# Residual additions moved to VectorE and four groups of tiles moved to other memory in a one-layer decoder step

## The chip, the cores and the metric

The kernel runs on one core of a Trainium2 chip. The metric is the device time of one execution in microseconds (us). A core has TensorE (PE, the matrix engine, whose weight loads are listed as PEld), VectorE (DVE), ScalarE (ACT), GpSimd (POOL) and SyncE (SP, which here only issues DMAs). Each engine works through its own queue in order, and an instruction that waits holds up everything behind it on that queue.

## The reference, cut to what matters

One layer of a decoder is computed for 1024 prompt rows and 64 sample rows (1088 rows of 1024 values). The parts around the change are the end of the mixer and the feed-forward block:

```python
x = x + rms_norm(merged @ w_out, norm_mix_post)          # first residual addition
h = rms_norm(x, norm_ffn_pre)
a = h @ w_ffn_a                                          # DFF = 4096 columns
ctx = concatenate([conv_buf, a], axis=1)                 # conv_buf: 2 rows of state
c = conv_b + sum(ctx[:, j:j + T] * conv_w[j] for j in range(3))
y = (silu(c) * (h @ w_ffn_b)) @ w_ffn_d
x = x + rms_norm(y, norm_ffn_post)                       # second residual addition
# the last two rows of ctx are outputs too: p_ffn_conv (prompt) and s_ffn_conv (8 samples)
```

All products are in float32 quality: each operand is split into a high and a low part, and three matmuls (high x high, low x high, high x low) make one product.

## The kernel before

`phase1` and `phase2` compute the three branches of the mixer and their merged sum, which is left as split tiles (`act_h`, `act_l`). `phase3`, `ffn`, `down_group` and `down` hold what the change touches. SBUF memory is given out by pools that are stacked from two sides. When a pool is closed, a later pool gets its memory, and a tile of the later pool waits for the last readers of the tiles that lay there. A pool with `bufs=n` gives out n copies of a tile in rotation. The order of the instructions on each queue is not the order of the program: a planner chooses it when the program is built (`schedule_with_timeline_sim=True`), by its own estimate of when each instruction is ready. Instructions that use a pool's tiles come, in that order, behind the instructions that use the pools whose memory it takes.

**The first weight rows.** `phase3` multiplies the merged sum by `w_out`. Its 8 blocks of 128 weight rows (k = 0 to 7) are loaded on SP (L1413) and split in two by `split` (L143 on ScalarE for the high part, L144 on VectorE for the low part). The raw rows of k = 0 and 1 go to `w_raw`, a tile with 2 copies in a pool (`wp`) that lives through the whole kernel. Those of k = 2 to 7 go to `pn_x` and `pn_y`, 2 copies each, of the pool `xp`. This pool takes memory in which the merged sum `macc` of `phase2` lay.

**The rows of the mixer's output.** The output is made in 9 tiles of rows, in the order 0 and 2 together, 1, 3, 4, 6, 5, 7, 8 (tile 8 holds the 64 sample rows). `sums` makes the matmuls of a tile (L1428, into `ps_u`, `ps_n`, `ps_d`), `norms` the rest: x is loaded into `pn_x` (L1439), squares are summed on ScalarE (L1443), `rstd` makes the factor (L160 to L165), VectorE multiplies (L1448), the residual is added (L1449), the row is stored (L1450), normalized again (L1452, L1454), and transposed on TensorE (L1459, read back at L1462). The two additions of a tile are on GpSimd for the tiles 0 to 6 and on VectorE for 7 and 8. The normalized x is written over the loaded x, so that a copy of `pn_x` is free for the next load only after the transposes.

**The up products and the state copies.** `ffn` makes both up products (L1628), in 16 steps of two column blocks, and writes their product to memory as `yd`. `down_first` loads and splits the first two blocks of the last product (weights L1733, y L1734). After the last step, two calls of `down_group` multiply these (L1782; the sample rows at L1774; L1788 adds to the sums, `act_h` and `act_l`). Then the state rows (`tail`) are transposed on TensorE (L1721), copied five times by VectorE into `tailT`, which has one copy (L1723), and stored by DMAs that GpSimd issues (L1724).

**The last product.** `down` opens the pool `dp`, which takes the memory of the closed pools of the up products. Its groups are one of 2 blocks (2 and 3) and seven of 4 blocks. `prep` gives a block its tiles and calls `down_part` (load the raw weight rows to `w_raw`, load y to `y_raw`, split both). For odd groups, the first one among them, y goes to `act_h1`/`act_l1`, and the first two blocks' weights go to `w_hi`/`w_lo`, which also hold the weights of blocks 0 and 1. For even groups y goes to `yh`/`yl` and the weights to `wd`, all of `dp`. `y_raw`, `gbf` and `sel` are always of `dp`. When the last group has finished a tile of 128 rows, `rows_done` makes the final norm of it (L1820 to L1825), the second residual addition (L1826; GpSimd for the prompt tiles 0 to 6, VectorE for the samples and tile 7) and the store.

Of the kernel before, what the change touches and what calls it, by code (L numbers as in the profile page):

```python
# [17 lines left out]
F32 = mybir.dt.float32  # L18
# [7 lines left out]
P = 128  # L26
D = 1024
SEQ = 1024
SB, ST = 8, 8
NS = SB * ST  # L30
# [89 lines left out]
class Builder:  # L120
# [1265 lines left out]
    def phase3(self, early):  # L1386

        tc, nc, I, O = self.tc, self.nc, self.I, self.O
        PS = bass.MemoryType.PSUM
        with ExitStack() as es:  # L1390
# [17 lines left out]
            wpt = lambda n, d=F32R: flat(self.wp.tile([P, 8, P], d, name=n))  # L1408
            wt = [wo.tile([P, D], F32R, name="w_row", bufs=10) for _ in range(10)]
            wk = []  # L1410
            for k in range(8):
                raw = wpt("w_raw", F32) if k < 2 else xp.tile([P, D], F32, name=("pn_x", "pn_y")[k % 2])
                self.shift_caches(nc.sync.dma_start(raw, I["w_out"][0][k * P:(k + 1) * P]))  # L1413
                wk.append((wpt("w_hi"), wpt("w_lo")) if k < 2 else wt[2 * (6 - k):2 * (6 - k) + 2] if k < 7 else (wpt("w_raw"), wpt("w_raw")))
                self.split(*wk[k], raw)
# [17 lines left out]
            def norms(i, ps, R, half):  # L1433

                a, e = ROWT[i]
                rows = e - a
                add = nc.vector if i >= 7 else nc.gpsimd
                x = xp.tile([P, D], F32, name="pn_x")[:rows]
                nc.sync.dma_start(x, self.xrows(a, e))  # L1439
                y = xp.tile([P, D], F32, name="pn_y")[:rows]  # L1440
                ss = self.sm.tile([P, 2], F32, name="pn_ss")[:rows]
                for u in range(2):
                    nc.scalar.activation(y[:, :512], ps[u], AF.Square, accum_out=ss[:, u:u + 1])  # L1443
                nc.vector.tensor_add(ss[:, 0:1], ss[:, 0:1], ss[:, 1:2])
                r = self.rstd(ss[:, 0:1], rows, D)
                for u in range(2):
                    v = slice(u * 512, (u + 1) * 512)
                    nc.vector.scalar_tensor_tensor(y[:, v], ps[u], r, gb[:rows, v], op0=ALU.mult, op1=ALU.mult)  # L1448
                    add.tensor_add(y[:, v], y[:, v], x[:, v])  # L1449
                nc.gpsimd.dma_start(self.x1d[a:e], y)  # L1450
                s2 = self.sm.tile([P, 1], F32, name="nrm_ss")[:rows]
                nc.scalar.activation(x, y, AF.Square, accum_out=s2)  # L1452
                r = self.rstd(s2, rows, D)
                nc.scalar.activation(x, y, AF.Copy, scale=r)  # L1454
                for c in range(8):
                    if c % 4 == 0:
                        pt = self.next_bank()
                    p = pt[:, c % 4 * P:c % 4 * P + rows]
                    nc.tensor.transpose(p, x[:, c * P:(c + 1) * P], self.ident[:rows, :rows])  # L1459
                    g = self.vec[:, VR_FFN + c:VR_FFN + c + 1]  # L1460
                    dst, src = (R[:, c], p.rearrange("p (h n) -> p h n", h=2)) if half is None else (R[:, c, half], p)
                    nc.scalar.activation(dst, src, AF.Copy, scale=g)  # L1462
# [7 lines left out]
            for j, (i, ps, _) in enumerate(tiles):  # L1470
                norms(i, ps, R02, j)
# [3 lines left out]
            for i, pl, nm in order:  # L1475
                ps, step = sums(i, pl, nm)
# [174 lines left out]
    def ffn(self, es, eu, pool, fs, stT):  # L1651
        tc, nc, I, O = self.tc, self.nc, self.I, self.O
# [4 lines left out]
        fp = pool(eu, "fp", 4)  # L1657
        W = SEQ + 2 + SB * 10
# [54 lines left out]
        self.down_start(pc)  # L1713
        for _ in range(2):
            self.down_group([self.aready.popleft()])
        for (j0, n, dst) in ((0, 2, O["p_ffn_conv"][0, 0]), (2, 16, O["s_ffn_conv"][0].rearrange("b j f -> (b j) f"))):
            d2 = dst.rearrange("j (r p) -> (j r) p", p=P)
            for a in range(0, n, 4):
                w = min(4, n - a)
                ps = self.down_bank()  # L1720
                nc.tensor.transpose(ps[:32 * w, :P], tail[:, j0 + a:j0 + a + w].rearrange("p j f -> p (j f)"), self.ident)  # L1721
                t = fs.tile([P, P], F32, name="tailT", bufs=1)
                nc.vector.tensor_copy(t[:32 * w], ps[:32 * w, :P])  # L1723
                nc.gpsimd.dma_start(d2[32 * a:32 * (a + w)], t[:32 * w])  # L1724
        eu.close()
        self.down(es, pool)

# [63 lines left out]
    def down(self, es, pool):  # L1791
        tc, nc, I, O = self.tc, self.nc, self.I, self.O
        dp = pool(es, "dp", 1, side="right")
        gb = dp.tile([P, D], F32, name="gbf")
        nc.sync.dma_start(gb, I["norm_ffn_post"][0].partition_broadcast(P))
        sel = dp.tile([P, NS], F32, name="sel")
        nc.vector.tensor_add(sel, self.ident[:, :NS], self.ident[:, NS:])
        held = {}

        def prep(g, j, fb):  # L1800

            if g % 2:
                if j == 0:
                    held[g] = [self.actp.tile([P, 4, D], F32R, name=f"act_{x}1") for x in "hl"]
                y = tuple(t[:, j] for t in held[g])
            else:
                y = tuple(dp.tile([P, D], F32R, name=n, bufs=4) for n in ("yh", "yl"))
            w = (self.wtile(self.wp, "w_hi"), self.wtile(self.wp, "w_lo")) if g % 2 and j < 2 else \
                tuple(dp.tile([P, D], F32R, name="wd", bufs=12) for _ in range(2))
            ys = dp.tile([P, 2, NS], F32R, name="ys", bufs=9)  # L1810
            return self.down_part(fb, self.wtile(self.wp, "w_raw", F32), w, dp.tile([P, NT], F32, name="y_raw", bufs=2), y, ys)

        def rows_done(src, rows, r0, dst, add):

            x, y = (t[:rows, len(done) % 4] for t in held["end"])
            done.append(r0)
            nc.sync.dma_start(x, self.x1d[r0:r0 + rows])
            ss = self.sm.tile([P, 2], F32, name="pn_ss")[:rows]
            for u in range(2):
                nc.scalar.activation(y[:, u * 512:(u + 1) * 512], src(u), AF.Square, accum_out=ss[:, u:u + 1])  # L1820
            nc.vector.tensor_add(ss[:, 0:1], ss[:, 0:1], ss[:, 1:2])  # L1821
            r = self.rstd(ss[:, 0:1], rows, D)
            for u in range(2):
                v = slice(u * 512, (u + 1) * 512)
                nc.vector.scalar_tensor_tensor(y[:, v], src(u), r, gb[:rows, v], op0=ALU.mult, op1=ALU.mult)  # L1825
                add.tensor_add(y[:, v], y[:, v], x[:, v])  # L1826
                nc.sync.dma_start(dst[:, v], y[:, v])

        done = []

        def samples_done():
            held["end"] = [self.actp.tile([P, 4, D], F32, name=f"act_{x}1") for x in "hl"]
            s = [dp.tile([P, 512], F32, name=f"smp{u}") for u in range(2)]
            fin = []
            for u in range(2):
                nc.scalar.activation(s[u], self.smp[u], AF.Copy)
                ps = self.down_bank(4)[:NS]
                nc.tensor.matmul(ps, sel, s[u], start=True, stop=True)
                fin.append(ps)
            rows_done(lambda u: fin[u], NS, SEQ, O["y_sample"].rearrange("b t d -> (b t) d"), nc.vector)  # L1840
        groups = [(2, 3)] + [tuple(range(a, a + 4)) for a in range(4, NFB, 4)]
        grp = [prep(1, j, fb) for j, fb in enumerate(groups[0])]
        for g, _ in enumerate(groups, 1):
            nxt = []
            todo = deque(groups[g] if g < len(groups) else ())

            def after(i):
                for _ in range(1 if len(grp) == 4 else 2):
                    if i % 2 == 0 and todo:
                        nxt.append(prep(g + 1, len(nxt), todo.popleft()))  # L1850
                if g == len(groups):
                    acc = self.acc[i]
                    rows_done(lambda u: acc[:, u * 512:(u + 1) * 512], P, i * P, O["y_prompt"][0, i * P:(i + 1) * P],
                              nc.vector if i == 7 else nc.gpsimd)
            self.down_group(grp, after, samples_done if g == len(groups) else lambda: None)
            grp = nxt

# [30 lines left out]
```

## Time and profile before

| what | us |
|---|---|
| median of 3 runs | 2800.94 (2800.14 to 2802.79) |
| the execution that was profiled | 2808.87 |
| its span in the profile | 2807.0 |

The profile describes one execution. Its times are counted from the start of the span. In a timeline row the columns are start, duration, engine (SPq is SP's queue), line, operation, output and inputs, shape and count; a bracket at the end tells how long the engine was idle before and what ended that. Rows with a count above 1 are merged, and their duration is that of the whole. TensorE's matmuls of 512 columns start some 0.23 us apart at its full clock.

### The profile page before, as it was taken

Reading aid. Unit: us, or ns where it says so; the run is one execution under the profiler, and the core shown is the slowest. Engines: PE = TensorE matmul, PEld = TensorE weight load, DVE = VectorE, ACT = ScalarE, POOL = GpSimd, SP = SyncE. Lnnn points to the kernel's source line nnn. Section 1 sums busy time; section 2 is a strip of 40 time slices with the busy share of each in tenths; the row PEclk is TensorE's granted clock in tenths of the full one; section 3 lists DMA queues with packets and bytes.
Section 4 is the critical chain, followed back from the end, with each engine's and each line's share of the span. In section 5 each row is a group of like instructions: output and inputs, shape, how many; then the busy total and the mean of one; then the engine's idle time right before and its main releaser. Section 6 shows DMA issues by size and latency. Waiting matters only on the chain. (4 is left out here: it accounts for less than half of the span.)

```text
span 2807.0 us, 45540 instructions
## 1 busy us (share of the span) xinstructions
PE 2661.6 (95%) x17822; PEld 2398.1 (85%) x17822; DVE 1651.0 (59%) x3944; ACT 1097.0 (39%) x2036; POOL 238.0 (8%) x367
## 2 busy tenths in 40 slices
PE   7989999899899999999999967999999999799998
PEld 6978888787787989999899747999999999588886
DVE  6346657557565754535358247777777777653435
ACT  5224526435355544444513355333333333221212
POOL 2110010000100000000000120100100100000002
PEclk9999999999999999999999988999999999899999
DMA  7456776867766333232475332332332332431303
GB/s 224 126 178 177 188 213 187 217 177 187 210 182 177 100 112 100 77 101 76 150 248 192 127 108 68 130 115 91 115 114 76 99 99 78 136 124 62 123 32 128
DMA packets 344552, 380.72 MB, mean 136 GB/s; under 512 B 57068, under 2 KB 295076, under 8 KB 343417
## 3 DMA queue, kind: packets, MB, share of 16 engines
q1 hardware_dynamic: 321808, 311.13, 36.8%
q0 software_dynamic: 22240, 65.63, 7.3%
q8 instruction: 140, 2.29, 0.3%
q10 hardware_dynamic: 288, 1.05, 0.1%
q14 instruction: 76, 0.61, 0.1%
HBM read 302.07 MB, written 123.46 MB: 152 GB/s over the span
## 5 line engine op out<-in xcount | busy, mean ns | idle before, releaser
L244 PE MATMUL ps_d<-act_h,w_hi 128*128 128x512 f32 (+2 forms) x1920 | 648.9, 338 | 8.3 <-DVE proj L832 6.8
L244 PE MATMUL ps_d<-act_l,w_hi 128*128 128x512 f32 (+2 forms) x1920 | 650.3, 339 | 0.0
L244 PE MATMUL ps_d<-act_h,w_lo 128*128 128x512 f32 (+2 forms) x1920 | 646.1, 337 | 0.0
L244 PEld LDWEIGHTS ps_d<-act_h,w_hi 128*128 128x128 f32 x1920 | 367.7, 192 | 37.1 <-DVE proj L832 7.5
L244 PEld LDWEIGHTS ps_d<-act_l,w_hi 128*128 128x128 f32 x1920 | 367.8, 192 | 30.0 <-issue 3.8
L244 PEld LDWEIGHTS ps_d<-act_h,w_lo 128*128 128x128 f32 x1920 | 367.6, 191 | 28.0 <-issue 2.8
L143 ACT ACTIVATE w_hi<-w_raw 128x1024 fp32r<-128x1024 f32 (+1 forms) x156 | 140.5, 903 | 275.2 <-PE ps_d L244 184.6
L144 DVE TENSOR_TENSOR w_lo<-w_raw,w_hi 128x1024 fp32r<-128x1024 f32 (+1 forms) x124 | 138.4, 1118 | 117.1 <-ACT w_hi L143 115.4
L1066 DVE CUSTOM_DVE_ANT_0 qb<-kc,qb 128x128 f32<-128x128 f32 x384 | 89.3, 287 | 101.2 <-DMA qb<-qrow 86.5
L1628 PE MATMUL ps_u<-Yh,w_hi 128*128 128x288 f32 (+1 forms) x512 | 103.7, 292 | 6.0 <-ACT Yh L143 6.0
L1628 PE MATMUL ps_c<-Yh,wx 128*128 128x288 f32 (+1 forms) x512 | 106.3, 289 | 0.0
L1628 PE MATMUL ps_u<-act_h,w_lo 128*128 128x288 f32 (+1 forms) x512 | 104.7, 289 | 1.0 <-DVE rs_v L160 1.0
L1628 PE MATMUL ps_d<-act_h,w_hi 128*128 128x288 f32 (+1 forms) x512 | 104.6, 293 | 0.7 <-DVE pn_y L1448 0.7
L1628 PE MATMUL ps_u<-Yh,wx 128*128 128x288 f32 (+1 forms) x512 | 102.4, 289 | 0.0
L1628 PE MATMUL ps_d<-act_h,w_lo 128*128 128x288 f32 (+1 forms) x512 | 101.6, 288 | 0.1
L1628 PE MATMUL ps_c<-act_h,wx 128*128 128x288 f32 (+1 forms) x512 | 101.4, 288 | 0.0
L244 PE MATMUL ps_d<-ohi,w_hi 128*128 128x256 f32 (+2 forms) x288 | 94.3, 329 | 2.5 <-ACT proj L1144 1.4
L244 PE MATMUL ps_d<-olo,w_hi 128*128 128x320 f32 (+2 forms) x288 | 94.6, 328 | 0.0
L244 PE MATMUL ps_d<-ohi,w_lo 128*128 128x320 f32 (+2 forms) x288 | 94.1, 327 | 0.0
L1144 ACT ACTIVATE proj<-ps_d,nbin 128x512 f32<-128x512 f32 (+2 forms) x96 | 53.3, 555 | 94.9 <-PE ps_d L244 94.9
L143 ACT ACTIVATE wx<-S 128x512 fp32r<-128x512 f32 x64 | 40.4, 632 | 124.9 <-PE ps_c L1628 124.9
L1628 PEld LDWEIGHTS ps_u<-Yh,w_hi 128*128 128x128 f32 x512 | 83.7, 192 | 6.2 <-ACT Yh L143 6.2
(638 smaller groups left out, 6365.6 us busy)
## 6 DMA issues: line engine op xcount, KB each, us to landing
w_raw<-in_w_in SPq DMA_DIRECT2D x80, 512.0 KB, 4.1
out_s_win<-in_cache_win_kv SPq DMA_DIRECT2D x40, 1016.0 KB, 7.0
kc<-in_cache_win_kv SPq DMA_DIRECT2D x80, 256.0 KB, 3.8
qb<-qrow SPq DMA_DIRECT2D x64, 256.0 KB, 4.8
kc<-in_cache_win_kv SPq DMA_DIRECT2D x128, 128.0 KB, 3.3
w_raw<-in_w_ffn_a SPq DMA_DIRECT2D x32, 512.0 KB, 3.8
w_raw<-in_w_ffn_b SPq DMA_DIRECT2D x32, 512.0 KB, 3.6
yd<-ext POOLq DMA_DIRECT2D x32, 512.0 KB, 4.8
```

What stands on the lines that cost most here:

```text
L143: self.nc.scalar.activation(hi, src, AF.Copy)
L144: self.nc.vector.tensor_sub(lo, src, hi.bitcast(F32))
L244: nc.tensor.matmul(ps, W[:, c], X(c), start=n == 0, stop=n == 3 * kb - 1)
L1066: nc.vector.tensor_tensor_reduce(q[:, j], k[:, j], q[:, j], 1.0, 0.0, ALU.mult, ALU.add, T[:, c:c + 1])
L1144: self.proj(col, lambda ps, a, e: nc.scalar.activation(y[:, a:e], ps, AF.Exp, bias=nb, scale=-1.0))
L1628: nc.tensor.matmul(p, w[:, c], self.side_b(t, b, x, c), start=new and m == 0, stop=m == 11, skip_group_check=not new)
```

## The change

It does four things. (1) The additions L1449 and L1826 are on VectorE for all tiles. (2) The raw rows of k = 2 and 3 of `w_out` go to `w_raw`. (3) The state copies go to five column ranges of one tile `ext` of the pool `fp`, whose four copies served the up products. (4) In `prep` the odd and even groups change roles, so that the first group's y and weights go to `yh`/`yl` and `wd` of `dp`, and the last group's to `act_h1`/`act_l1`; `rows_done` then takes `yh`/`yl` in place of parts of `act_h1`/`act_l1`.

```diff
-                raw = wpt("w_raw", F32) if k < 2 else xp.tile([P, D], F32, name=("pn_x", "pn_y")[k % 2])
+                raw = wpt("w_raw", F32) if k < 4 else xp.tile([P, D], F32, name=("pn_x", "pn_y")[k % 2])
...
-                add = nc.vector if i >= 7 else nc.gpsimd
...
-                    add.tensor_add(y[:, v], y[:, v], x[:, v])
+                    nc.vector.tensor_add(y[:, v], y[:, v], x[:, v])
...
+        tails = fp.tile([P, W], F32, name="ext")
+        o = 0
...
-                t = fs.tile([P, P], F32, name="tailT", bufs=1)
-                nc.vector.tensor_copy(t[:32 * w], ps[:32 * w, :P])
-                nc.gpsimd.dma_start(d2[32 * a:32 * (a + w)], t[:32 * w])
+                t = tails[:32 * w, o:o + P]
+                o += P
+                nc.vector.tensor_copy(t, ps[:32 * w, :P])
+                nc.gpsimd.dma_start(d2[32 * a:32 * (a + w)], t)
...
-            if g % 2:
+            if g % 2 == 0:
                 if j == 0:
                     held[g] = [self.actp.tile([P, 4, D], F32R, name=f"act_{x}1") for x in "hl"]
                 y = tuple(t[:, j] for t in held[g])
             else:
                 y = tuple(dp.tile([P, D], F32R, name=n, bufs=4) for n in ("yh", "yl"))
-            w = (self.wtile(self.wp, "w_hi"), self.wtile(self.wp, "w_lo")) if g % 2 and j < 2 else \
+            w = (self.wtile(self.wp, "w_hi"), self.wtile(self.wp, "w_lo")) if g % 2 == 0 and j < 2 else \
                 tuple(dp.tile([P, D], F32R, name="wd", bufs=12) for _ in range(2))
...
-            x, y = (t[:rows, len(done) % 4] for t in held["end"])
-            done.append(r0)
+            x, y = (dp.tile([P, D], F32, name=n, bufs=4)[:rows] for n in ("yh", "yl"))
...
-                add.tensor_add(y[:, v], y[:, v], x[:, v])
+                nc.vector.tensor_add(y[:, v], y[:, v], x[:, v])
```

## Rows read from the trace of the kernel before

**Rows 1.** The page: busy time, share of the span and instructions of each engine.
```profile
PE 2661.6 (95%) x17822; PEld 2398.1 (85%) x17822; DVE 1651.0 (59%) x3944; ACT 1097.0 (39%) x2036; POOL 238.0 (8%) x367
```

**Rows 2.** Stretches: us, busy PE, PEld, DVE, ACT, POOL, granted clock, DMA share, GB/s.
```profile
1661.00:1690.00 29.00, 11.33 (x51) 8.66 (x50) 21.84 (x46) 20.20 (x52) 9.90 (x6) 0.65 0.53 188
...
2412.50:2425.00 12.50, 0.05 (x1) 0.00 (x0) 2.25 (x5) 3.48 (x5) 1.10 (x2) 0.64 0.56 182
2425.00:2441.00 16.00, 11.01 (x26) 7.50 (x27) 9.24 (x13) 5.66 (x9) 1.62 (x3) 0.54 0.54 183
...
2757.00:2795.00 38.00, 37.80 (x167) 30.96 (x165) 29.96 (x66) 12.64 (x43) 17.87 (x12) 1.00 0.47 153
```

**Rows 3.** Timeline of DVE, SP, ACT and PE at the first weight rows.
```profile
1535.93 1.22 DVE L144 TENSOR_TENSOR w_lo<-w_raw,w_hi 128x1024 fp32r<-128x1024 f32 x1
1544.47 1.23 DVE L144 TENSOR_TENSOR w_lo<-w_raw,w_hi 128x1024 fp32r<-128x1024 f32 x1
...
1546.16 0.33 SPq L1405 DMA_DIRECT2D gb<-in_norm_mix_post  x1
1546.54 0.42 SPq L1413 DMA_DIRECT2D pn_x<-in_w_out  x1
...
1552.21 1.06 ACT L143 ACTIVATE w_row<-pn_x 128x1024 fp32r<-128x1024 f32 x1 [7.22 <-DMA pn_x<-in_w_out]
...
1553.32 0.79 PE L1428 MATMUL ps_u<-w_row,act_h 128*128 128x512 f32 x1 [4.25 <-ACT w_row L143]
1558.18 0.63 PE L1428 MATMUL ps_d<-w_row,act_l 128*128 128x512 f32 x1
1560.54 0.40 PE L1428 MATMUL ps_u<-w_row,act_l 128*128 128x512 f32 x1
```

**Rows 4.** Timeline of POOL, PE and DVE at the first residual additions.
```profile
1607.94 2.53 POOL L1449 TENSOR_TENSOR pn_y<-pn_y,pn_x 128x512 f32<-128x512 f32 x2 [21.05 <-DMA pn_x<-in_x_prompt]
1628.32 3.28 POOL L1449 TENSOR_TENSOR pn_y<-pn_y,pn_x 128x512 f32<-128x512 f32 x2 [16.99 <-DVE act_l L144]
1665.16 6.26 POOL L1449 TENSOR_TENSOR pn_y<-pn_y,pn_x 128x512 f32<-128x512 f32 x2 [25.47 <-DVE w_lo L144]
1679.64 2.52 POOL L1449 TENSOR_TENSOR pn_y<-pn_y,pn_x 128x512 f32<-128x512 f32 x2 [7.36 <-DVE pn_y L1448]
...
1679.40 0.69 PE L1459 MATMUL ps_t<-ident,pn_x 128*128 128x128 f32 x2 [12.50 <-ACT pn_x L1454]
...
1688.68 1.29 DVE L1449 TENSOR_TENSOR pn_y<-pn_y,pn_x 128x512 f32<-128x512 f32 x2 [0.25 <-DMA pn_x<-in_x_prompt]
```

**Rows 5.** Timeline of SP, ACT, DVE and PE at the start of the last product.
```profile
2414.20 0.33 SPq L1733 DMA_DIRECT2D w_raw<-in_w_ffn_d  x1
2414.69 1.05 SPq L1795 DMA_DIRECT2D gbf<-in_norm_ffn_post  x1
2415.83 0.86 SPq L1734 DMA_DIRECT2D y_raw<-yd  x2
...
2411.86 1.06 ACT L143 ACTIVATE w_hi<-w_raw 128x1024 fp32r<-128x1024 f32 x1 [9.65 <-issue]
2423.94 1.06 ACT L143 ACTIVATE act_h<-y_raw 128x1024 fp32r<-128x1024 f32 x1 [4.35 <-DMA y_raw<-yd]
...
2424.71 0.29 DVE L1723 COPY tailT<-ps_c 128x128 f32<-128x128 f32 x1 [7.84 <-DMA out_s_ffn_conv<-tailT]
2432.38 1.22 DVE L144 TENSOR_TENSOR act_l<-y_raw,act_h 128x1024 fp32r<-128x1024 f32 x1
...
2425.05 0.80 PE L1782 MATMUL ps_d<-w_hi,act_h 128*128 128x512 f32 x1 [12.50 <-DVE tailT L1723]
2433.66 0.79 PE L1782 MATMUL ps_d<-w_hi,act_l 128*128 128x512 f32 x1 [2.74 <-DVE act_l L144]
```

**Rows 6.** The last rows: sums by line, then timeline rows of PE and DVE.
```profile
L1821 DVE TENSOR_TENSOR pn_ss<-pn_ss 128x1 f32<-128x1 f32 x8 | 6.9, 868 | 3.3 <-ACT act_l L1820 3.3
L165 DVE TENSOR_TENSOR rs_r<-rs_r,rs_u 128x1 f32<-128x1 f32 x8 | 1.3, 159 | 0.3
...
2794.41 0.39 PE L1782 MATMUL ps_c<-wd,yh 128*128 128x512 f32 x1
2797.23 0.68 DVE L1788 TENSOR_TENSOR act_l<-act_l,ps_c 128x512 f32<-128x512 f32 x1
```

More of the change, by code (lines that the diff above doesn't have):

```diff
@@ L1811, in prep, with rows_done @@
             return self.down_part(fb, self.wtile(self.wp, "w_raw", F32), w, dp.tile([P, NT], F32, name="y_raw", bufs=2), y, ys)
-        def rows_done(src, rows, r0, dst, add):
-            x, y = (t[:rows, len(done) % 4] for t in held["end"])
-            done.append(r0)
+        def rows_done(src, rows, r0, dst):
+            x, y = (dp.tile([P, D], F32, name=n, bufs=4)[:rows] for n in ("yh", "yl"))
             nc.sync.dma_start(x, self.x1d[r0:r0 + rows])
@@ L1825, in rows_done @@
                 nc.vector.scalar_tensor_tensor(y[:, v], src(u), r, gb[:rows, v], op0=ALU.mult, op1=ALU.mult)
-                add.tensor_add(y[:, v], y[:, v], x[:, v])
+                nc.vector.tensor_add(y[:, v], y[:, v], x[:, v])
                 nc.sync.dma_start(dst[:, v], y[:, v])
-        done = []
         def samples_done():
-            held["end"] = [self.actp.tile([P, 4, D], F32, name=f"act_{x}1") for x in "hl"]
             s = [dp.tile([P, 512], F32, name=f"smp{u}") for u in range(2)]
@@ L1839, in samples_done @@
                 fin.append(ps)
-            rows_done(lambda u: fin[u], NS, SEQ, O["y_sample"].rearrange("b t d -> (b t) d"), nc.vector)
+            rows_done(lambda u: fin[u], NS, SEQ, O["y_sample"].rearrange("b t d -> (b t) d"))
         groups = [(2, 3)] + [tuple(range(a, a + 4)) for a in range(4, NFB, 4)]
@@ L1852, in after @@
                     acc = self.acc[i]
-                    rows_done(lambda u: acc[:, u * 512:(u + 1) * 512], P, i * P, O["y_prompt"][0, i * P:(i + 1) * P],
-                              nc.vector if i == 7 else nc.gpsimd)
+                    rows_done(lambda u: acc[:, u * 512:(u + 1) * 512], P, i * P, O["y_prompt"][0, i * P:(i + 1) * P])
             self.down_group(grp, after, samples_done if g == len(groups) else lambda: None)
```

## The prediction, made before the changed kernel ran

> **What bounds the kernel now.** I read the page first. TensorE is busy for 2661.6 of 2807.0 us [rows 1], so it sets the time nearly everywhere and an edit pays only where TensorE stands still or runs at its lower clock. The page's slices and then the table of stretches show that this happens where one stage hands over to the next. I then went through TensorE's timeline for its idle brackets and followed each to what released it. Three hand-overs and the end of the kernel lie in the code that changes.
>
> At the first weight rows TensorE has used up the blocks k = 0 and 1 of w_out and waits 4.25 us for block 2 [rows 3]. Its raw rows were asked for at 1546.54, behind gb at 1546.16, because both lie where the merged sum lay, and landed shortly before ScalarE's split at 1552.21. After the wait TensorE is at its lower level (1.2 GHz): from 1553.32 to 1558.60 it does 12 matmuls 0.43 us apart, where 0.23 is the full pace.
>
> In the rows of the mixer's output TensorE waits 12.50 us for the normalized x of tile 6 [rows 4], and in the stretch 1661 to 1690 it is busy for 11.33 of 29 us, while VectorE is for 21.84 and ScalarE for 20.20 [rows 2].
>
> At the start of the last product it waits 12.50 us, and again 2.74 us [rows 5]; two more waits between them make 2.2 us. In 2425 to 2441 it does 26 matmuls, at a clock of 0.54 [rows 2], which at 0.23 us each are 6.0 us of work. So the hand-over loses 12.5 + (16 - 6.0) = 22.5 us. Two things cause it. The y of the first group is asked for at 2415.83, because SP stood until 2414.20 at a weight load (that of block 5) whose raw tile was not split before 2411.86, which in turn had to wait for the products of block 1 to let go of w_hi and w_lo. And VectorE copies the state rows through one tile: each copy waits for the store of the one before, up to 7.84 us, so that the low part of y comes only at 2432.38 [rows 5].
>
> At the end the last matmul is over at 2794.80, and VectorE adds it to the sums only at 2797.23 [rows 6]; 9.8 us of norm and store follow, up to the span's end.
>
> **The change part by part.** *First weight rows.* Block 2 can now be loaded once block 0 is split, at 1535.93 + 1.22 = 1537.15, and block 3 from 1544.47 + 1.23 = 1545.70 [rows 3]. No other load is displaced on SP: the next one, gb, is issued at 1546.16 anyhow. Block 2 then lies ready before TensorE wants it at about 1549.1, and its matmuls for three row tiles (18 at 0.23, 4.1 us) last to 1553.2. Block 3 is issued ahead of gb, and if it takes as long as block 2 did (1546.54 to 1552.21, 5.7 us) it can be split from 1551.4, the high part by 1552.5. Gone are the 4.25 us and 12 x (0.43 - 0.23) = 2.4 us: **6.6**. Bounds: 2.5, if block 3 lands 4 us late, and 6.6.
>
> *First additions.* Fourteen additions on GpSimd, 2.5 us for most pairs, become as many on VectorE at 1.29 a pair [rows 4]. Where TensorE has other work (tiles 0, 2, 1) I cost them at nothing: sums of later tiles cover them; without that cover it would be 1.29 each. On the path is tile 6. Its pair took 6.26 us, because VectorE was busy beside it, and the 12.50 us wait follows from it; with 1.29 up to 5.0 go. What is late next is the factor, which already stands in the queues of ScalarE and VectorE among splits of the up weights, so I take 3.0. Tile 5's pair gives back 0.7 (the two products and additions take 2.7 together, where they took 3.4), tile 3's 0.3. Together **4**. Bounds: -3 (VectorE has 7 x 1.2 = 8.4 us more, of which I let a third fall on the path, since it is busy for three quarters of 1661 to 1690) and 8. Whenever an addition waits for its x, all that is queued on VectorE waits too: factors, products that free PSUM banks, splits. I cost that at nothing since the pair of tile 7, which is on VectorE already, waited 0.25 us [rows 4].
>
> *State copies.* Each copy costs VectorE 0.29 us [rows 5] and none waits for a store, so five end some 1.5 us after the transposes, about 2414, instead of at 2430. The tile's own memory held products whose stores were issued by 2391, so nothing hides there.
>
> *First group.* Its weights and y are now tiles of dp. In the trace whatever uses dp (y_raw, gbf, sel, wd) stands behind the last state copy on its queue, so the low splits of all four tiles come after 2414: 4 x 1.2 us, the last at 2419. Block 3's weights can still not be early: by the pools' sizes they fall on tiles that hold y of block 1 until about 2411.6. But nothing stands before the y loads on SP any more, since the weight loads of blocks 4 and 5 now come after these splits. The y loads can then start while blocks 0 and 1 are still multiplied, and y's high part is due at about 2414.5 on ScalarE. TensorE is idle from 2412.55 to then, 2.0 us, and some 3.0 more until the low parts are there; 0.5 to 1.5 for a lower clock. That leaves 6.5 of 22.5: **16**. The second group must be ready earlier too. Before, its y loads were spread over 16 us; now they start that much earlier, and VectorE has 6 blocks' splits (6 x 2.4) and 16 sums (16 x 0.6), 24 us, in the 26 us up to 2440. It just fits. Bounds: 5, if the y loads still land after 2422 and only the later waits and the lower clock go, and 20.
>
> *Last additions.* Seven pairs, 8.4 us, go to VectorE, which is busy for 29.96 of 38 us there [rows 2]. In return the small sum L1821 has its way free: it takes 0.87 us on average beside GpSimd's additions, where the like operation L165 takes 0.16 [rows 6], so 8 x 0.7 = 5.7 us go. The net 2.7 us can fall into VectorE's idle time (it waits for ScalarE several times a tile), and then the 2.4 us lag at the end shrinks, or they can come on top. I take a gain of **1**, between -2.7 and 3. The Trainium skill says, in SBUF — State Buffer, section Who interferes with whom, that a VectorE instruction with two SBUF inputs and a GpSimd instruction that reads SBUF exclude each other, the later one waiting in full; rows 6 agree, and by that rule alone the term would be 0.7 for the last tile. Its page Perfetto Trace Analysis, section Optimizing Scalar/DVE Operations, speaks against the edit: a saturated VectorE may be relieved by handing work to GpSimd. By that the term would be -2.7.
>
> The sum is 6.6 + 4 + 16 + 1 = 27.6. Against the profiled execution (2808.87, of which 2807.0 is the span and 1.9 lies around it) that is 2781.3. This execution is 7.9 us above the median of the runs shown; taken off their median, 2800.94, it is **2773.3**, rounded to 2774. With all lower ends the gain is 2.5 - 3 + 5 - 2.7 = 1.8 (2799), with all upper ones 37.6 (2763).
>
> **The rivals.** *The last product's hand-over stays.* For: block 3's weights are bound as before, and every split of the first group now stands behind the copies. If the y loads are placed behind gbf or the copies' stores, they land as late as before, after 2422. Against: SP no longer meets a load that waits for a split. Then this term is 5, the additions and the end are 0, and the gain is 11.6: 2789.
>
> *VectorE stands in the waits for x.* GpSimd's additions waited 21.05, 16.99 and 25.47 us for their x [rows 4], 63.5 in all, and it cost nobody anything. If the planner, expecting x earlier, puts an addition ahead of ready work, VectorE waits in its place. The place is tiles 3 and 6, after which TensorE has no sums left to cover: 17.0 + 25.5 = 42.5 us, against the 23.6 of the other terms: 2800.94 - 23.6 + 42.5 = 2820. It decides once more than 27 us of these waits are met. Against: the wait of 0.25 us at tile 7.
>
> *The edits do little.* If the planner's new order opens as much elsewhere as it closes, the time is within 5.6 us of 2801; I see no row for it.
>
> **How the numbers follow.** Forecast, 2766 to 2781: 0.66. Hand-over stays, 2782 to 2794: 0.18. VectorE in the waits, 2807 or more: 0.07. Little: 0.04. More than forecast (upper ends), below 2766: 0.05. A measurement of this kernel can tell some 0.2%, 5.6 us, from no change. So faster 0.89, same 0.04, slower 0.07. The range 2764 to 2792 takes in the forecast, most of the first rival and part of the upper ends, and leaves out less than 0.2.
>
> **What would show it.** Right: no wait above 1 us at block 2 of w_out, and a clock of 1.0 there; tile 6's wait below 10 us; the first y loads of dp issued before 2412 on the old time scale, state copies some 0.3 us apart, TensorE's wait before the first group below 4 us; L1821 near 0.16 us. Wrong: VectorE rows at L1449 with brackets of 10 us or more that a load of pn_x ended; y_raw loads still issued after the copies; a new wait at the second group; the last VectorE sum more than 3 us behind the last matmul.

## The result and the profile after

The changed kernel takes 2769.62 us (median of 4 runs, 2768.37 to 2774.73) beside 2801.86 for the kernel before in the same runs: a ratio of 0.9884, with a 95% interval of 0.9864 to 0.9904. The forecast was 2774, between 2764 and 2792. A second series of the same kernel (below) gave 0.9899 (0.9881 to 0.9917). The two differences are 32.2 and 27.0 us. The profiled execution took 2770.02 us, 2767.8 of it the span.

The page's busy times of the changed kernel, to be laid beside [rows 1]:

```profile
PE 2652.2 (96%) x17822; PEld 2391.7 (86%) x17822; DVE 1654.2 (60%) x3972; ACT 1096.3 (40%) x2036; POOL 196.2 (7%) x339
```

TensorE does the same 17822 matmuls in 9.4 us less busy time, and its share rises from 95% to 96%. The rest is idle time that went. GpSimd loses its 28 additions.

Five stages can be cut out of TensorE's timeline by its own rows: up to the first product of w_out, from there to the first product of the up weights with Yh (Yh and Yl are the high and low part of differences of the normalized rows; the product stands behind a wait of 5.6 to 7.1 us that ScalarE's Yh ends), to the end of the up products, to the last matmul, and to the span's end. In the two profiled executions:

| stage, us | before | after | difference |
|---|---|---|---|
| up to the first product of w_out | 1538.77 | 1531.19 | -7.6 |
| w_out and the norms, up to the Yh products | 183.44 | 170.72 | -12.7 |
| up products | 666.22 | 666.63 | +0.4 |
| last product | 406.37 | 388.14 | -18.2 |
| after the last matmul | 12.20 | 11.12 | -1.1 |

The first stage is no part of the change: TensorE's order of work is the same there in all kernels of this study. Over its 14 profiled executions that stage varies from 1527.78 to 1541.41 us. The stages behind it repeat far better, and this is why the experiments are read stage by stage. In the kernels that leave a stage unedited, w_out and the norms take 182.3 to 183.4 (five kernels, mean 182.9), the last product 403.4 to 406.4 (five, mean 404.7), the tail, which is the stage after the last matmul, 12.1 to 12.2 (five). Four traces hold the changed kernel's w_out and norms as they are: 170.55, 170.72, 170.89 and 172.46. By the means of the unedited kernels the change gains 12.2 + 16.5 + 1.1 - 0.4 = 29.4 us, and the forecast's sum was 27.6.

The stretches of after, in the columns of [rows 2]. The first is the start of w_out, with the same stretch of before beneath it; the others answer to those of [rows 2]:

```profile
1531.19:1561.91 30.72, 30.72 (x139) 25.03 (x138) 11.84 (x16) 10.27 (x15) 0.00 (x0) 1.00 0.56 218
...
1646.00:1675.00 29.00, 12.73 (x65) 9.27 (x63) 25.26 (x55) 22.17 (x61) 1.60 (x3) 0.71 0.58 199
2392.67:2405.17 12.50, 9.31 (x40) 7.38 (x41) 9.63 (x16) 6.53 (x10) 2.69 (x5) 1.00 0.70 245
2405.17:2421.17 16.00, 16.00 (x72) 13.19 (x71) 15.97 (x24) 9.36 (x14) 0.00 (x0) 1.00 0.84 272
2718.88:2756.88 38.00, 37.80 (x163) 30.24 (x162) 30.93 (x75) 13.10 (x44) 0.00 (x0) 1.00 0.47 156
```
```profile
1538.77:1569.49 30.72, 26.47 (x108) 21.14 (x107) 11.90 (x15) 8.96 (x10) 0.00 (x0) 0.89 0.58 221
```

At w_out TensorE is never idle any more, and does 139 matmuls where it did 108. In the rows of the mixer's output it still stands for more than half the stretch, now with VectorE busy for 25.26 of 29 us. At the last product's start the clock stays at 1.00, where it was 0.64 and 0.54.

### The profile page after: what moved, and what is told of

The parts are those of the page before. It is cut to its first block, busy times and chain, and to the rows that moved or that the text cites. A ratio compares the mean times of both kernels' runs of the same rounds, so it can differ in the third digit from the quotient of the medians.

```text
span 2767.8 us, 45536 instructions
## 1 busy us (share of the span) xinstructions
PE 2652.2 (96%) x17822; PEld 2391.7 (86%) x17822; DVE 1654.2 (60%) x3972; ACT 1096.3 (40%) x2036; POOL 196.2 (7%) x339
## 4 chain that ended last, share of the span: by engine, by line
PE 79%; DMA 7%; issue 7%; DVE 3%; ACT 2%; SPq 1%; POOL 0%; DVEq 0%; POOLq 0%; ACTq 0%
PE ps_d L244 30%; PE ps_u L1627 10%; PE ps_c L1627 7%; PE ps_d L1627 7%; PE ps_u L1784 4%; PE ps_d L1784 4%; PE ps_c L1784 4%; DMA qb<-qrow 2%; DMA kt<-kb 1%; PE ps_d L1428 1%; PE ps_u L1428 1%; PE ps_n L1428 1%; PE ps_c L1776 1%; DMA kc<-in_cache_win_kv 1%; DMA comb<-ocomb 1%
## 5 line engine op out<-in xcount | busy, mean ns | idle before, releaser
L244 PEld LDWEIGHTS ps_d<-act_h,w_lo 128*128 128x128 f32 x1920 | 367.4, 191 | 27.6 <-issue 2.5
```

The lines of the kernel that those rows point to most:

```text
L244: nc.tensor.matmul(ps, W[:, c], X(c), start=n == 0, stop=n == 3 * kb - 1)
```

## The experiments

All kernels below are timed against the kernel before in the same runs, and each was profiled once. Behind "Measured" stands the ratio of the times with its 95% interval, then the lengths of stages from the one trace; "the mean" is that of the unedited kernels above.

**Which of the two edits opens the last product?** One kernel has the state copies alone, one the exchange of odd and even groups alone, one both and nothing else.

```diff
+        tails = fp.tile([P, W], F32, name="ext")
...
-                t = fs.tile([P, P], F32, name="tailT", bufs=1)
+                t = tails[:32 * w, o:o + P]
```

> The kernel before with the state copies alone moved to ranges of one tile. Theory A (each of the two edits at the last product opens one of two doors that stand one behind the other): the copies end some 1.5 us after the transposes, about 2414 on the old time scale instead of 2430, so the three later waits (0.45, 1.76 and 2.74 us) go and the lower clock after them is shorter; but the y loads of the first group still stand behind the weight load of block 5 on SP, the high part of y is ready at 2425 as before, and the 12.5 us wait stays. Gain 5 to 9 us, time 2792 to 2797. Rival B (the copies alone were what the hand-over waited for, as the releaser of the 12.5 us wait says): that wait falls below 4 us too, gain 14 to 19, time 2782 to 2787. Rival C: no gain, since y is late anyway.

Measured: 0.9969 (0.9959 to 0.9979), 8.7 us; the last product's stage is 395.66, 9.0 less than the mean. This is theory A. The timeline of the kernel with the copies alone:

```profile
2423.67 0.80 PE L1785 MATMUL ps_d<-w_hi,act_h 128*128 128x512 f32 x1 [10.62 <-ACT act_h L143]
...
2413.21 0.47 DVE L1726 COPY ext<-ps_u 64x128 f32<-64x128 f32 x2
...
2415.14 0.28 DVE L1726 COPY ext<-ps_d 128x128 f32<-128x128 f32 x1
...
2416.16 1.03 SPq L1737 DMA_DIRECT2D y_raw<-yd  x2
...
2422.56 1.06 ACT L143 ACTIVATE act_h<-y_raw 128x1024 fp32r<-128x1024 f32 x1 [2.50 <-DMA y_raw<-yd]
```

The last copy now starts at 2415.14, with one split between it and the others, and no later wait is left. But the first y is asked for at 2416.16 and split at 2422.56, and TensorE waits 10.62 us for it. In the trace of before the releaser of the 12.50 us wait was a state copy [rows 5]; here the same wait stands with the copies long done. Both were late together, and the row had named only the one that came last.

```diff
-            if g % 2:
+            if g % 2 == 0:
...
-            x, y = (t[:rows, len(done) % 4] for t in held["end"])
+            x, y = (dp.tile([P, D], F32, name=n, bufs=4)[:rows] for n in ("yh", "yl"))
```

> The kernel before with the roles of odd and even groups changed alone; the state copies go through the one old tile. Theory A: y of the first group is loaded early, but the copies wait for their stores as before, the first PSUM banks come free at 2425 and the low parts of y, behind the last copy on VectorE, come after 2431. The wait of about 12 us stays, named after the copies. Gain 0 to 4, time 2797 to 2801. Rival B (y was what was late, the copies only stood beside it): the wait falls below 6 us, gain 10 or more, time below 2791.

Measured: 0.9989 (0.9975 to 1.0003); the stage is 401.63, 3.0 less than the mean and 1.8 less than the shortest of the unedited kernels, which spread over 3.0 us themselves. The gain is that of theory A. In one point neither text is right: the 12 us wait did not stay, it broke up. The timeline of the kernel with the groups alone:

```profile
2391.53 0.85 SPq L1734 DMA_DIRECT2D y_raw<-yd  x2
...
2412.61 0.50 PE L1782 MATMUL ps_d<-wd,yh 128*128 128x512 f32 x1 [1.32 <-ACT yh L143]
...
2415.72 0.80 PE L1782 MATMUL ps_u<-wd,yh 128*128 128x512 f32 x1 [2.38 <-DVE tailT L1723]
...
2423.35 0.79 PE L1782 MATMUL ps_d<-wd,yh 128*128 128x512 f32 x1 [1.76 <-DVE tailT L1723]
2426.88 0.80 PE L1782 MATMUL ps_d<-wd,yl 128*128 128x512 f32 x1 [2.74 <-DVE yl L144]
...
2415.38 0.29 DVE L1723 COPY tailT<-ps_u 128x128 f32<-128x128 f32 x1 [3.64 <-DMA out_p_ffn_conv<-tailT]
```

y is asked for at 2391.53, 21 us before it is used, and the first product starts after 1.32 us. Then each PSUM bank in turn is held by a state copy that waits for a store, four times, and the low part of y waits behind the last of them. The first matmul after each of these waits lasts some 0.8 us, where the one at 2412.61 took 0.50.

> The kernel before with both edits of the last product's start, the copies and the groups, and without the other two. Theory A: the two gain together more than the sum of each alone: 16 to 19 us, time 2782 to 2785, TensorE's two waits there below 2 us each, as in the changed kernel (1.31 and 1.88). Rival (part of the 18.2 us seen in the changed kernel at this place comes from the additions or from another order of work): 10 to 14 us, time 2787 to 2791.

Measured: 0.9943 (0.9929 to 0.9957), 16.0 us; the stage is 388.11, 16.5 less. One edit gives 9.0 and the other 3.0, but both together give 16.5. That is 4.5 more than the sum, and more than the 3.0 us of spread: the doors stand one behind the other. The changed kernel's stage is 388.14, so nothing at this place comes from the other edits.

**The first weight rows.** One kernel has `k < 4` alone, one `k < 3`.

```diff
-                raw = wpt("w_raw", F32) if k < 2 else xp.tile([P, D], F32, name=("pn_x", "pn_y")[k % 2])
+                raw = wpt("w_raw", F32) if k < 4 else xp.tile([P, D], F32, name=("pn_x", "pn_y")[k % 2])
```

> The kernel before with the raw rows of blocks 2 and 3 of w_out alone in the long-lived tile. Theory: the 4.25 us wait and the 12 slow matmuls go, 6.6 us at the first weight rows, and nothing is given back later: 2794 to 2796. Rival (the rows after it are bound by their chains and by x, not by when the products start): up to 4 us come back as longer waits for the normalized rows, 2797 to 2801.

Measured: 0.9984 (0.9974 to 0.9994), 4.5 us; w_out and the norms take 177.10 us, 5.8 less than the mean. Neither text is quite right: what was gained at the blocks came back in part, and something else was gained further on. TensorE reaches the products of the sample rows 85.2 us after its first product of w_out, where it took 92.9. But there it waits 6.78 us, where it waited 4.43:

```profile
1627.90 0.69 PE L1428 MATMUL ps_n<-w_hi,act_h 128*64 128x512 f32 x1 [6.78 <-DVE pn_y L1448]
...
1608.28 0.16 DVE L1444 TENSOR_TENSOR pn_ss<-pn_ss 128x1 f32<-128x1 f32 x1 [1.40 <-ACT pn_y L1443]
...
1625.63 0.14 DVE L160 TENSOR_SCALAR rs_v<-nrm_ss 128x1 f32<-128x1 f32 x1
1625.69 0.14 DVE L160 TENSOR_SCALAR rs_v<-pn_ss 128x1 f32<-128x1 f32 x1
...
1627.10 1.41 DVE L1448 SCALAR_TENSOR_TENSOR pn_y<-ps_n,rs_r,gb 128x512 f32<-128x512 f32 x2
...
1620.23 3.25 POOL L1449 TENSOR_TENSOR pn_y<-pn_y,pn_x 128x512 f32<-128x512 f32 x2 [16.61 <-DVE act_l L144]
```

The bank belongs to tile 4. Its sum of squares is ready at 1608.44, but the next step of its factor (the second L160) stands on VectorE right behind the same step of tile 3's second norm, which comes after GpSimd's addition of tile 3 at 1620.23. So 17 us pass in which the queue's order holds the bank, since VectorE's part is otherwise ready. Behind tile 6, on the other hand, its transposes and those of tile 8 are 24.4 us apart instead of 26.9. This happens with either of the edits in this stage (24.4 with the first additions alone, too) and with none of the others (27.0 to 27.2), so it is put down to the new order that the planner chose; it was not tested by itself.

> As the kernel with the first weight rows alone, but only block 2 of w_out has its raw rows in the long-lived tile; block 3 comes, as block 2 did, behind the release of the merged sum. Theory A (one block of work, 4.1 us, covers the load that follows): block 3's raw rows land at 1552 as block 2's did, its high part is ready about when TensorE wants it, and the gain is that of two blocks within 2 us: 2794 to 2797. Rival (block 3 lands 4 us after it is wanted, the lower bound of the forecast's first term): the wait moves to block 3, with the lower clock behind it, and the gain is 2.5 us or less: 2798 to 2801.

Measured: 0.9974 (0.9962 to 0.9986), 7.3 us; the stage takes 176.23, 6.7 less. This is theory A. The timeline of the kernel with block 2 alone:

```profile
1552.30 1.06 ACT L143 ACTIVATE w_row<-pn_y 128x1024 fp32r<-128x1024 f32 x1 [5.85 <-DMA pn_y<-in_w_out]
...
1553.62 0.40 PE L1428 MATMUL ps_u<-w_row,act_h 128*128 128x512 f32 x1
```

Block 3's rows are asked for at 1547.04, its high part is split from 1552.30 to 1553.36, and TensorE begins with it at 1553.62 without a wait. One more block of work was cover enough, with 0.3 us to spare.

**The first additions alone.**

```diff
-                add = nc.vector if i >= 7 else nc.gpsimd
+                add = nc.vector
```

> The kernel before with the first residual additions alone on VectorE. Theory: the forecast's 4 us, between 3 and 6; the wait for tile 6 is 10 to 10.5 us instead of 12.5, and VectorE waits less than 3 us in all for x: 2795 to 2798. Rival (VectorE, busy for 25.3 of 29 us in this stretch of the changed kernel, has become the bound there, and the gain seen came with the earlier weight rows): within 2 us of no change, 2799 to 2803.

Measured: 0.9989 (0.9977 to 1.0002), which the time alone can't tell from no change; but w_out and the norms take 177.25 us, 5.7 less than the mean and outside the 1.1 us over which the unedited kernels spread. The wait for tile 6 is 9.71 us. The rival falls: the gain is there without the earlier weight rows. With both edits the changed kernel takes 170.72 and, again, 170.89: 12.1 together, 11.5 as a sum of the two.

**The last additions alone, and what slowed the small sum.**

```diff
-                              nc.vector if i == 7 else nc.gpsimd)
+                              nc.vector)
```

> The kernel before with the last residual additions alone on VectorE. Theory: 1 us, too little for the time to show; in the trace the small sum of squares takes 0.16 us on average instead of 0.79, and the end follows the last matmul after 11 us instead of 12.2. Rival (the small sum was slow for another reason than GpSimd's additions): it stays at 0.7 or more, and the end is 1 to 3 us later.

Measured: 1.0003 (0.9990 to 1.0016); the tail is 11.10. The small sums of this kernel by line (count, busy us, mean ns), to be laid beside the first row of [rows 6]:

```profile
L1821 DVE TENSOR_TENSOR pn_ss<-pn_ss 128x1 f32<-128x1 f32 (+1 forms) x9 | 1.4, 155 | 5.0 <-ACT act_l L1820 5.0
```

The nine sums take 0.155 us on average, where the nine of before take 0.79 (0.868 without the first, the row in [rows 6]). What GpSimd must do to slow them was asked in the changed kernel with work that nobody uses:

```diff
+                if r0 < 3 * P:
+                    for _ in range(3):
+                        nc.gpsimd.memset(x[:, v], 0.0)
+                elif r0 < 6 * P:
+                    for _ in range(3):
+                        nc.gpsimd.tensor_copy(x[:, v], y[:, v])
```

> The changed kernel with idle work on GpSimd beside the last norms, whose results nobody uses: behind the final additions of tiles 0 to 2 six fills of 128x512, which read nothing, behind those of tiles 3 to 5 six copies of 128x512, which read one tile. Theory (GpSimd's reading is what holds up VectorE's small sums with two inputs): the small sums stay at 0.16 us for the tiles beside the fills and take 0.5 us or more for those beside the copies. Rival (any GpSimd work does, or only work with two inputs does): both are slow, or both stay at 0.16.

Measured (one run, 2787.71 us, with a tail of 17.06, so this work is not free): beside fills the small sums keep their time, beside copies they don't. Timeline rows of GpSimd and VectorE:

```profile
2748.15 6.23 POOL L1831 MEMSET yh<- 128x512 f32 x12 [5.16 <-PE ps_u L1784]
...
2753.73 0.16 DVE L1822 TENSOR_TENSOR pn_ss<-pn_ss 128x1 f32<-128x1 f32 x1 [0.73 <-ACT yl L1821]
...
2759.36 2.10 POOL L1834 COPY yh<-yl 128x512 f32<-128x512 f32 x2 [0.61 <-DVE yl L1827]
...
2760.90 0.56 DVE L1822 TENSOR_TENSOR pn_ss<-pn_ss 128x1 f32<-128x1 f32 x1
...
2766.56 0.15 DVE L1822 TENSOR_TENSOR pn_ss<-pn_ss 128x1 f32<-128x1 f32 x1
...
2770.00 0.34 DVE L165 TENSOR_TENSOR rs_r<-rs_r,rs_u 128x1 f32<-128x1 f32 x1
```

The sum at 2753.73 lies within the fills (2748.15 to 2754.38) and takes 0.16, as does another at 2752.19. The one at 2760.90 begins within the copies and takes 0.56, and the one at 2766.56 in a pause of GpSimd takes 0.15. Only this one sum met copies, but so did four other steps of 128x1 with two inputs (L163 and L165), the one at 2770.00 among them. Each of the five ends 0.01 us after the copy that ran when it began. Steps with one input (L160 and L164) keep their 0.15 us beside copies. The trace of before shows the same beside GpSimd's additions, in which six of the nine last sums take 0.93 to 1.25 us:

```profile
2771.07 1.73 POOL L1826 TENSOR_TENSOR act_l<-act_l,act_h 128x512 f32<-128x512 f32 x1 [2.96 <-DVE act_l L1825]
2771.57 1.25 DVE L1821 TENSOR_TENSOR pn_ss<-pn_ss 128x1 f32<-128x1 f32 x1
```

All six, like this one, end 0.01 or 0.02 us after the addition that ran when they began. So it is shown that such a step is slowed while GpSimd reads and not while it fills, and that what it loses is the rest of the GpSimd instruction that it meets.

**A version that is cut differently.** The product with the norm's weight can be taken before the factor is known; behind the factor then stands one pair of VectorE instructions, not two.

```diff
-                    nc.vector.scalar_tensor_tensor(y[:, v], ps[u], r, gb[:rows, v], op0=ALU.mult, op1=ALU.mult)
-                    nc.vector.tensor_add(y[:, v], y[:, v], x[:, v])
+                    nc.vector.tensor_mul(y[:, v], ps[u], gb[:rows, v])
...
+                    nc.vector.scalar_tensor_tensor(y[:, v], y[:, v], r, x[:, v], op0=ALU.mult, op1=ALU.add)
```

> The changed kernel with the two residual steps cut differently: the product with the norm's weight is taken before the factor is known, and one instruction then multiplies by the factor and adds x. VectorE has as many large instructions as before, but only one pair of them, not two, follows the factor. Theory (what is late in the changed kernel is the chain through the factor): the end follows the last matmul 1.3 us earlier, the PSUM bank wait of 5.27 us shrinks by 2 to 4, tile 6's by 1: 4 to 6 us less than the changed kernel, 2764 to 2766. Rival (in the rows after w_out VectorE's queue as a whole is late, not the chain): only the end gains, 2768 to 2769.

Measured: 0.9894 (0.9876 to 0.9912). By its time it is no faster than the changed kernel (0.9884 and 0.9899), and its 2773.48 us lie above what either text expects. The tail is 8.76, 2.4 less than in the changed kernel; w_out and the norms take 169.18, 1.5 less, which is within the spread of the changed kernel's four traces. The bank wait of 5.27 us (in the changed kernel, before the products of the sample rows) is gone altogether and the last product of w_out ends 106.02 us after the first, where the changed kernel took 115.28. But 7.7 of these 9.3 us are lost again: TensorE stands before the up weights.

```profile
1652.54 0.58 PE L1629 MATMUL ps_u<-Yh,w_hi 128*128 128x256 f32 x1 [8.36 <-ACT w_hi L143]
...
1638.61 0.93 SPq L1580 DMA_DIRECT2D w_raw<-in_w_ffn_a  x2
```

The raw up weights are asked for at 1638.61, when the last products of w_out let go of their tile, and the work that needs them follows 14 us later. So the rival is right in its sum for this stage, which gains little; as to the reason, the chain that TensorE waits for starts with that load, and VectorE is less busy in the 29 us behind the last product of w_out than in the changed kernel (21.86 us for 25.26). What an earlier load would give was not tried. The same kernel again, the changed kernel, and the new cut at the end alone were then run side by side.

> The changed kernel once more, to stand beside the two kernels that follow in the same runs: 0.988 of the kernel before, and the same lengths of each stage within 1.5 us: 115.3 us from the first product of w_out to the last, 55.4 to the wait before the Yh products, 388.1 from the end of the up products to the last matmul, 11.1 after it.

Measured: 0.9899 (0.9881 to 0.9917), and 170.89, 388.11 and 11.11 us for the stages.

> The changed kernel with the new cut of the residual step at the end of the kernel alone. Theory (the chain through the factor is what is late after the last matmul): the tail is 8.8 us, as in the kernel with both new cuts, in place of 11.1, all other stages are as in the changed kernel, 2.4 us less. Rival: VectorE is the bound there and the work only moves ahead of the last matmul, so that the last sum comes later: no gain.

Measured: 0.9886 (0.9866 to 0.9906). The tail is 8.79 us, the stages before it 170.55 and 388.14. By its stages this version is 2.3 us ahead of the changed kernel; the times, 2773.37 beside 2776.38, can't tell them apart.

> The kernel with both new cuts once more. Theory from its first trace (the rows after w_out gain 9.3 us where the products run and lose 7.7 behind them, since the raw up weights then come last): 1.5 us there and 2.4 at the end, 3 to 5 us less than the changed kernel. Rival: the 9.3 us gained and 7.7 lost are chance of one execution, and the two kernels are equal but for the end.

Measured: 0.9892 (0.9873 to 0.9912), with 105.99 us for the products of w_out, 64.02 from there to the Yh products and a tail of 8.77. So the gain and the loss are no chance: against the changed kernel of the same series they are 9.6 and 8.7 us. Together they make 0.9 us, which these traces can't tell from nothing; the tail's 2.3 is what is left.

## Why the prediction was right, and where not

The forecast's mechanism held and no rival came about. Its sum was closer than its parts: within three of the four terms misses of opposite sign met, and that is luck. Its terms, in its order, with the stage means as measure:

**First weight rows: 6.6 forecast, 5.8 alone.** At the blocks all went as worked out, even a little better: 31 matmuls more in the same 30.72 us, 7.1 us at 0.23. Rows of after that answer to [rows 3]:

```profile
1537.33 1.05 ACT L143 ACTIVATE w_row<-w_raw 128x1024 fp32r<-128x1024 f32 x1
1541.98 1.06 ACT L143 ACTIVATE w_row<-w_raw 128x1024 fp32r<-128x1024 f32 x1 [3.61 <-DMA w_raw<-in_w_out]
...
1541.34 0.40 PE L1428 MATMUL ps_u<-w_row,act_h 128*128 128x512 f32 x1
...
1545.54 0.39 PE L1428 MATMUL ps_u<-w_row,act_h 128*128 128x512 f32 x1
```

The high part of block 2 is ready 3.0 us before its first product, that of block 3 2.5 us before its own. What the step left out is what stands behind: 2.4 us came back at the bank of tile 4, and about as much (2.5) was gained behind tile 6, which the step had not named either. The lower bound of 2.5 rested on a late block 3, and the kernel with block 2 alone shows that not even a block 3 loaded as late as before would have cost that.

**First additions: 4 forecast, 5.7 alone, and 12.1 with the rows where 10.6 were forecast.** Of tile 6's wait 2.0 us went, forecast 3.0 (the mark of less than 10 us was missed at 10.45; in the second series it was met, at 9.79). Rows of VectorE and TensorE in after, to be laid beside [rows 4]:

```profile
1616.01 1.29 DVE L1448 TENSOR_TENSOR pn_y<-pn_y,pn_x 128x512 f32<-128x512 f32 x2
...
1649.72 1.28 DVE L1448 TENSOR_TENSOR pn_y<-pn_y,pn_x 128x512 f32<-128x512 f32 x2
...
1655.60 0.15 DVE L160 TENSOR_SCALAR rs_v<-nrm_ss 128x1 f32<-128x1 f32 x1
...
1660.65 1.15 ACT L1453 ACTIVATE pn_x<-pn_y,rs_r 128x1024 f32<-128x1024 f32 x1 [2.37 <-DVE rs_r L165]
...
1661.85 0.69 PE L1458 MATMUL ps_t<-ident,pn_x 128*128 128x128 f32 x2 [10.45 <-ACT pn_x L1453]
```

Tile 6's addition is done at 1651.00, and its normalized x comes at 1661.80. In between the square waits for ScalarE (at 1652.82) and each small step of the factor waits in VectorE's queue among splits and sums of the up weights: L160 at 1655.60, the last step at 1660.46. The forecast had named the factor in these queues as next, and it took still more than allowed for.

The term was larger all the same. Alone, the additions take 2.8 us off tile 6's wait; the wait for the bank of tile 4 falls by 0.9 (from 4.43 to 3.49), where 0.3 had been forecast for tile 3, whose pair takes 1.29 in after instead of 3.28; and behind tile 6 the new order brings 2.6 us, of which the forecast had only the 0.7 of tile 5's pair (3.4 us from its product to the end of its addition before, 2.6 in after). The rows alone bring nearly the same behind tile 6, so that it counts once in the 12.1. From the kernel with the rows alone to the changed kernel the stage is 6.4 us shorter: 1.6 up to the products of the sample rows, whose bank tile 4 holds, 1.1 more up to the last product of w_out, 2.6 up to tile 6's transposes and 1.0 behind them.

The rival of VectorE standing in the waits for x had a chance of 0.07. The waits that it met, from the summary of line L1448 in after:

```profile
  DMA pn_x<-in_x_prompt: 2.3, 2
  DMA pn_x<-in_x_sample: 1.3, 1
```

They are 3.6 us in all, of the 63.5 that GpSimd had stood, and 1.8 of them fall on an addition that was moved (tile 1); tiles 7 and 8 were on VectorE already. Two of the brackets in [rows 4] name a VectorE split, not the load; but tile 6's x landed at 1665.00 in before, 0.16 us before its addition, so the forecast was right to call these waits waits for x. In the new order the additions stand behind ready work.

**State copies and first group: 16 forecast, 16.5.** Rows of SP, ScalarE, VectorE and TensorE in after, to be laid beside [rows 5]:

```profile
2372.86 1.19 SPq L1736 DMA_DIRECT2D y_raw<-yd  x2
...
2391.92 1.06 ACT L143 ACTIVATE wd<-w_raw 128x1024 fp32r<-128x1024 f32 x1 [9.42 <-PE ps_d L1784]
2392.89 1.04 ACT L143 ACTIVATE yh<-y_raw 128x1024 fp32r<-128x1024 f32 x1
...
2392.84 0.47 DVE L1725 COPY ext<-ps_u 64x128 f32<-64x128 f32 x2
...
2393.98 0.51 PE L1784 MATMUL ps_d<-wd,yh 128*128 128x512 f32 x1 [1.31 <-ACT yh L143]
...
2397.50 0.50 PE L1784 MATMUL ps_d<-wd,yl 128*128 128x512 f32 x1 [1.88 <-DVE yl L144]
```

Every step of it can be read there. The y loads follow gbf at 2372.86, 19 us before the state rows' transposes, since no weight load that waits for a split stands before them. Block 3's weights are split only at 2391.92, when the tiles that held y of block 1 come free, and y's high part is split behind them on ScalarE, at 2392.89. The five copies follow each other without a wait, some 0.2 us apart. TensorE waits 1.31 us for the high part and then 1.88 for the low part; 2.0 and 3.0 had been forecast, and the 0.5 to 1.5 for a lower clock did not come. With 3.2 us left of the 22.5, the term would have been 19.3. The two executions give 18.2, and 16.5 against the mean, since the last product of the one that was read was 1.7 us longer than the mean of the kernels that leave it alone. So what is left was forecast too large and the loss before too large as well; 1.1 us of the latter stay open (the 22.5 rests on a count of 26 matmuls at 0.23). That VectorE would just keep up with the second group (24 us of work in 26) was right: it is busy for 15.97 of the 16 us from 2405.17 on, and TensorE for all 16.

**Last additions: 1 forecast, 1.1.** The parts, however, were mis-sized. Rows of after, to be laid beside [rows 6]:

```profile
2756.29 0.39 PE L1784 MATMUL ps_c<-wd,act_h 128*128 128x512 f32 x1
...
2756.71 0.69 DVE L1790 TENSOR_TENSOR act_l<-act_l,ps_c 128x512 f32<-128x512 f32 x1 [0.98 <-PE ps_c L1784]
...
2757.95 1.41 DVE L1826 SCALAR_TENSOR_TENSOR yl<-act_l,rs_r,gbf 128x512 f32<-128x512 f32 x2
2759.28 0.15 DVE L1822 TENSOR_TENSOR pn_ss<-pn_ss 128x1 f32<-128x1 f32 x1
2759.35 1.28 DVE L1827 TENSOR_TENSOR yl<-yl,yh 128x512 f32<-128x512 f32 x2
2760.56 0.14 DVE L160 TENSOR_SCALAR rs_v<-pn_ss 128x1 f32<-128x1 f32 x1
```

The last sum now follows the last matmul at once, so the whole lag of 2.4 us went, not a part of it, and the small sum of tile 7 takes 0.15 for 0.93. But the squares of tile 7 are known at 2758.16, and the small sum stands behind tile 6's products until 2759.28, its next step behind tile 6's additions until 2760.56: 2.2 us given back. The kernel with the new cut at the end shows it from the other side, with 2.3 us less there. The exchange of the groups also gives the final norm other tiles, and the two kernels that have it without the additions have tails of 11.75 and 11.78; with the additions moved the tail is 11.1 with or without it.

Two rules of the Trainium skill were weighed. The one in SBUF — State Buffer, section Who interferes with whom, agrees with the runs: the small sums with two inputs end with the GpSimd instruction that they meet, and fills, which read nothing, do no harm. The advice of Perfetto Trace Analysis, section Optimizing Scalar/DVE Operations, would have made the last term -2.7; it was +1.1, with VectorE's busy time in the last 38 us up from 29.96 to no more than 30.93. The same section goes on to say that VectorE and GpSimd share a read port, so that offloading between those two might not help; the forecast left that out, and these runs agree with it.

## What to carry to other kernels

Where one engine waits, list everything that is not ready at that moment before costing an edit: the releaser in the profile is only what came last, and here two edits that gave 9.0 and 3.0 us alone gave 16.5 together. An elementwise step given to a second engine may be paid for by small dependent steps of the first; compare their duration beside that work and without it, one by one, since each loses what is left of the instruction it meets. And cost a hand-over to its end: earlier weights bring the work earlier only as far as the next bank or buffer that is bound to another chain.

## What was not expected of the hardware

The first 1530 us, the same work in the same order in all 14 profiled executions, take between 1527.78 and 1541.41 us, while the last product takes 388.09 to 388.46 in all that have both of its edits (seven executions). An effect of 5 us that the medians can't tell from no change (0.9989, 0.9977 to 1.0002) is plain in the stage where it arises.

A VectorE sum of 128x1 took 0.16 us beside GpSimd fills of 128x512, 0.56 beside a GpSimd copy, and 0.93 to 1.25 beside GpSimd additions (six in before). The price is neither the sum's own work nor a share of the reading: every slow step ended 0.01 or 0.02 us after the copy or addition that ran when it began. It goes the other way too: tile 6's first addition on GpSimd took 5.04 us in before (1665.16 to 1670.20), where the median of the fourteen is 1.28, and ended 1.1 us after the last of an unbroken run of VectorE instructions with two inputs (until 1669.08).
